# Macaron conformer / RG-LRU layer: a 128-column split at the entry of 256-column matmul runs, a fixed order for the first casts with idle matmuls on TensorE, and the quarter copies moved to a chain of lower priority

## The chip, the cores and the metric

The kernel runs on one core of one Trainium2 chip, as one launch. The metric is the device time of one execution in microseconds (us), median over runs. A separate profiled execution gives the trace; its span leaves out what lies before the first and behind the last instruction. Engines are named as in the profile: PE (TensorE matmul), PEld (TensorE weight load), DVE (VectorE), ACT (ScalarE), POOL (GpSimd), SP (the engine that issues most DMAs).

## The reference

One decoder layer on x of 512 tokens by 1024 features, float32, with three residual steps and a last norm:

```python
def swiglu_ffn(x, w_gate, w_up, w_down):
    return (jax.nn.silu(x @ w_gate) * (x @ w_up)) @ w_down

x = x + 0.5 * swiglu_ffn(rmsnorm(x, ffn1_norm), ...)     # 1024 -> 2816 -> 1024
x = x + hybrid_mixer(rmsnorm(x, mix_norm), ...)          # one 1024 -> 2048 input product
x = x + 0.5 * swiglu_ffn(rmsnorm(x, ffn2_norm), ...)
y = rmsnorm(x, final_norm)
```

The mixer splits its 2048 columns into four blocks of 512: value and gate of a causal depthwise convolution of width 31 (then a LayerNorm over channels and a silu), and input and gate of a linear recurrence over time (a convolution of width 4, two block-diagonal gates, a scan). Both halves go through one 1024 x 1024 output product.

## The kernel before

**Precision.** Every large product is made of three products in fp32r, a shorter float format of TensorE. An operand is split into `hi`, its value rounded to fp32r (a cast on ACT), and `lo`, the rest (a subtraction on DVE), and the sum is hi·hi + hi·lo + lo·hi. So each weight slab of 128 x 1024 that arrives by DMA (`raw`) costs a cast (line 203) and a subtraction (line 212) before PE can use it (`hl`), and each normed activation is transposed on PE (line 348, tile `ptr`), cast on ACT to `h_hi` (line 353) and subtracted on DVE to `h_lo` (line 359).

**Stages.** Both feed-forward parts have 22 feature tiles j of 128 features. The first two are computed in two halves of 256 tokens (`early_units`, called A and B in the code), because the norm of the first 256 tokens is ready first; each half is 24 matmuls of 256 columns into `pgate` and 24 into `pup` (line 305). Then, in the first part only, tile 2 is computed over all 512 tokens. The tiles behind that are computed by a seven-product scheme over quarters of the operands (`seven_units`, line 314): gate and up weights are one 2 x 2 block matrix, tokens and features of the input the other, and seven block products of 12 matmuls with 256 columns each (tiles `px`, `pz`, `pw`) do the work of eight. It needs sums of the input's quarters (`quarters`, lines 363 to 377, and `sums`, line 381; tiles `a`, `s`, `sx`) and sums of the weight blocks (lines 226 to 230, tile `tt`). Tiles are in groups of 8, 8 and 6; behind each group comes the down product in matmuls of 512 columns (lines 520 to 522), and behind its first slab stand 12 matmuls of 256 columns that were held back from the last tile (`late`). The mixer's input product (`zc_units`) begins with two column blocks in halves of 256 tokens and goes on with 512 columns.

**Order.** The work is a list of units. `run` goes through the list; for each unit it first issues what lies ahead by fixed distances (`AHEAD`: loads 8 slabs ahead, casts 4, subtractions 3), then the unit's matmuls, then one step of every side chain (norms, sums of quarters), then the unit's evacuation. The framework then orders each engine's queue by priority, in which `high_priority(offset=...)` moves a piece forward; `keep_in_program_order` pins an instruction to the place where it is written. Each engine runs its queue strictly in order. A norm is a chain (`norm_chain`): squares with a running sum on ACT (line 324), two small operations on POOL (lines 325 and 328), the scaling on DVE (line 340 for the first norm, where the gain is broadcast by a matmul with one row, `g`, line 893; line 334 for the later ones), then transposes, casts, subtractions and, for the two feed-forward norms, the copies for the quarters' sums. Tokens are in four tiles t of 128; the first norm handles t = 0 and 1 ahead of the list and t = 2 and 3 in a chain.

Of the kernel before, what the change touches and what calls it, by code (L numbers as in the profile page):

```python
# [8 lines left out]
F32 = mybir.dt.float32  # L9
# [19 lines left out]
BESIDE = (4, 5, 6, 9, 11, 13, 15, 18, 20)  # L29
ASIDE = 16  # L30
TAPS = 31
PR_NORM = 800
# [18 lines left out]
class Slab:  # L51
    def __init__(self, src=None, split=None, home=None, off=0):
        self.src, self.split, self.home, self.off = src, split, home, off


# [17 lines left out]
def layer_kernel(ctx: ExitStack, tc, x, gains, w_g1, w_u1, w_d1a, w_d1b, w_in,  # L73
# [119 lines left out]
    def slab_hi(s):  # L193
        if isinstance(s, Block):
            block_hi(s)
            return
        if s.home is not None:
            s.hi, s.lo = s.home()
        else:
            hl = hl_tile(s.off)  # L200
            s.hi, s.lo = hl[:, 0:D], hl[:, D:2 * D]
        if s.split is None:
            S.copy(s.hi, s.raw)  # L203
        elif s.home is not None:
            nc.sync.dma_start(s.hi.bitcast(F32), s.split[:, 0, :])
            nc.sync.dma_start(s.lo.bitcast(F32), s.split[:, 1, :])
        else:
            nc.sync.dma_start(hl.bitcast(F32).rearrange("p (s d) -> p s d", s=2), s.split)

    def slab_lo(s):  # L210
        if s.split is None:
            V.tensor_sub(s.lo, s.raw, s.hi.bitcast(F32))  # L212
            dve(1.15)


# [24 lines left out]
    def run(units):  # L240
# [8 lines left out]
        for i, u in enumerate(units):  # L249
            while used < len(order) and first[order[used]] <= i:  # L250
                used += 1
            for stage in range(3):
                while put[stage] < min(used + AHEAD[stage], len(order)):
                    s = order[put[stage]]
                    if stage == 0:
                        slab_load(s)
                    elif stage == 1:
                        if live >= HL_BUFS and put[1] >= used and s.home is None:
                            break
                        slab_hi(s)  # L260
                        live += s.home is None
                    else:
                        if put[2] >= put[1]:
                            break
                        slab_lo(s)
                    put[stage] += 1
# [32 lines left out]

    def mm_feat(ps, s, t0, n):  # L300
        hi = s.hi.rearrange("p (k f) -> p k f", k=KT)
        lo = s.lo.rearrange("p (k f) -> p k f", k=KT)
        for i, (w, h) in enumerate(((hi, h_hi), (hi, h_lo), (lo, h_hi))):
            for k in range(KT):
                PE.matmul(ps, w[:, k, :], h[:, k, t0:t0 + n],  # L305
                          start=(i == 0 and k == 0), stop=(i == 2 and k == KT - 1))

    def mm_block(ps, b, a, first):  # L310
        (whi, wlo), (hhi, hlo) = b, a
        for i, (w, h) in enumerate(((whi, hhi), (whi, hlo), (wlo, hhi))):
            for k in range(4):
                PE.matmul(ps[:, 0:HT], w[:, k * P:(k + 1) * P], h[:, k, :],  # L314
                          start=(first and i == 0 and k == 0), stop=(i == 2 and k == 3),
                          skip_group_check=not first)

# [3 lines left out]
    def norm_stats(t):  # L321
        xn = slot([P, D], "xn")
        ss = sp.tile([P, 16], F32, name=nm("ss"), tag="ss", bufs=4)
        S.activation(xn, xt[t], AF.Square, scale=1.0 / 32.0, accum_out=ss[:, 0:1])
        ins = G.tensor_scalar_add(ss[:, 0:1], ss[:, 0:1], RMS_EPS)
# [5 lines left out]
    def norm_scale(t, xs, g):  # L331
# [6 lines left out]
        for oh in range(2):  # L338
            sl = slice(oh * 512, (oh + 1) * 512)
            V.scalar_tensor_tensor(out=xn[:, sl], in0=xt[t][:, sl], scalar=ss[:, 1:2],  # L340
                                   in1=g[oh], op0=ALU.mult, op1=ALU.mult)

    def transposed(t, xs):
        pts = []
        for hf in range(2):
            pt = bank("ptr").rearrange("p (a b) -> p a b", a=4)
            for k in range(4):
                ins = PE.transpose(pt[:, k, :], xs[0][:, (hf * 4 + k) * P:(hf * 4 + k + 1) * P],
                                   ident)
                if pinned[0]:  # L350
                    tc.keep_in_program_order(ins)
            dst = (slice(None), slice(hf * 4, hf * 4 + 4), slice(t * P, (t + 1) * P))
            S.copy(h_hi[dst], pt)
            pts.append((pt, dst))
        return pts

    def transposed_lo(pts):
        for pt, dst in pts:
            V.tensor_sub(h_lo[dst], pt, h_hi[dst].bitcast(F32))
            dve(0.66)  # L360


    def quarters(t, pts, q):
# [4 lines left out]
        if t < 2:  # L368
            S.copy(q["a11"][at], p0)
            S.copy(q["a12"][at], p1)  # L370
        else:
# [4 lines left out]
        if t == 3:  # L376
            chains.append((PR_COMB, sums(q)))


# [19 lines left out]

    def norm_chain(ts, g, key=None, q=None):  # L400
        xs = [norm_stats(t) for t in ts]
        for t, x_ in zip(ts, xs):
            norm_scale(t, x_, g)
        yield 1
        for t, x_ in zip(ts, xs):
# [3 lines left out]
            if q is not None:  # L409
                quarters(t, p, q)  # L410
        if key is not None:
# [7 lines left out]

    def ffn_units(acts, j, g, u_, parts):  # L420
        off = ASIDE if len(parts) == 2 else 0
        sg_, su_ = Slab(g, off=off), Slab(u_, off=off)
        box = {}

        def product(key, s, t0, n):
            box[key] = bank("p" + key)
            mm_feat(box[key][:, :n], s, t0, n)

# [12 lines left out]
        for t0, n in parts:  # L441
            us = 5.44 * n / 512
            out_.append(Unit([sg_], us, lambda t0=t0, n=n: product("gate", sg_, t0, n),
                             lambda t0=t0, n=n: gate_out(t0, n), n == T))
            out_.append(Unit([su_], us, lambda t0=t0, n=n: product("up", su_, t0, n),
                             lambda t0=t0, n=n: up_out(t0, n), n == T))
# [4 lines left out]

    def seven_units(acts, j, g, u_, q):
        pair = {"gate": g, "up": u_}
# [6 lines left out]
        def product(to, b, a, first):  # L460
# [3 lines left out]
            sl = slice(i * HALF, (i + 1) * HALF)  # L464
            mm_block(box[to], (blk.hi[:, sl], blk.lo[:, sl]), q[a], first)

# [47 lines left out]
    def early_units(acts, wg, wu, between):  # L514
        e = [ffn_units(acts, j, wg[j], wu[j], [A, B]) for j in range(2)]
        return e[0][:2] + e[1][:2] + between + e[0][2:] + e[1][2:]

# [81 lines left out]
    def zc_units(c, parts):  # L599
# [4 lines left out]
        def product(key, s, t0, n):  # L604
            box[key] = bank("pz")
            mm_feat(box[key][:, :n], s, t0, n)

# [259 lines left out]
    def softplus_consts():  # L867
# [4 lines left out]
        V.tensor_max(e, lam, na)  # L872
        S.activation(e, e, AF.Exp, scale=-1.0)
        V.tensor_scalar_add(s, e, 2.0)
# [13 lines left out]

    row1 = sp.tile([1, P], F32, name="row1", tag="sg", bufs=2)
    V.memset(row1, 1.0)  # L890
    g1ps = [bank("g1") for _ in range(2)]
    for oh in range(2):
        PE.matmul(g1ps[oh], row1, grow[:, cols(oh)], start=True, stop=True)
    gains_of = {}
# [33 lines left out]
    def rest_of_x():  # L928
        for t in (2, 3):
            nc.sync.dma_start(xt[t], x[t * P:(t + 1) * P, :])  # L930
        chains.append((PR_FIRST, norm_chain((2, 3), g1ps, "h11", q1)))

# [8 lines left out]
    def ffn(a0, wg, wu, wd, q, plain, between=()):  # L941
# [8 lines left out]
        for gi, n in enumerate(GROUPS):  # L950
            for i in range(n):
# [9 lines left out]
                m = seven_units(acts[gi], i, wg[j], wu[j], q)  # L961
                m[4].aside = j in BESIDE
# [14 lines left out]
    e = early_units(a1, w_g1, w_u1, wait("h11"))  # L977
    u = e[:1] + do(rest_of_x) + e[1:]
    u += do(lambda: sides.append(split_ahead(for_later, ws_in + ws_out)))
# [121 lines left out]
```

## Time and profile before

| | |
|---|---|
| median of 3 runs | 871.55 us (870.31 to 871.9) |
| profiled execution, its own time | 874.41 us |
| its span | 872.4 us |
| PE busy | 849.3 us, 97% |
| DVE busy | 638.0 us, 73% |
| ACT busy | 425.6 us, 49% |
| DMA | 139.12 MB, mean 159 GB/s |

PE is busy nearly throughout, so what counts is how long its matmuls take and where it waits. Two things are to be kept in mind. A matmul's row in the timeline shows its start and a length that overlaps with the next one: the cost of a matmul in a dense run is the distance of its start to the next start, not its length. And the row "PEclk" is the clock that the throttle granted.

The list of engine queues that is shown beside the profile's rows tells which instruction stands where in its engine's queue; it has no times.

### The profile page before, as it was taken

What the parts mean: (1) busy time and instruction counts of PE and PEld (TensorE: products, weight loads), DVE (VectorE), ACT (ScalarE), POOL (GpSimd) and SP (SyncE); (2) the same over time, 40 slices, a digit from 0 to 9 for tenths busy, and PEclk for the clock granted to TensorE, in tenths of its full rate; (3) what the DMA queues carried; (4) which work ended last, traced back from release to release, by engine and by line L of the source; (5) the groups of instructions that cost most, each with busy time, mean ns of one, the idle gap of its engine ahead of it and who ended that gap; (6) DMA issues with size and microseconds to landing.
All of it is one profiled execution on the core that took longest, in us unless ns stands there. A gap on an engine that the chain in (4) does not pass through costs nothing.

```text
span 872.4 us, 13745 instructions
## 1 busy us (share of the span) xinstructions
PE 849.3 (97%) x5568; PEld 772.7 (89%) x5568; DVE 638.0 (73%) x899; ACT 425.6 (49%) x677; POOL 89.6 (10%) x112
## 2 busy tenths in 40 slices
PE   7999999999999999999996999999999999999996
PEld 5999988999889998998783889999889999899985
DVE  5989765997668984569897669796547994558844
ACT  7656533556435652435742545555225654135633
POOL 2000010000110000209820010000000000000001
PEclk9999999999999999999997999999999999999999
DMA  7536895555885569655451021234312335223312
GB/s 283 150 138 241 286 323 212 179 184 171 293 308 196 191 234 369 218 201 185 146 193 48 26 72 51 96 121 125 120 49 95 111 110 166 74 73 98 104 43 96
DMA packets 36721, 139.12 MB, mean 159 GB/s; under 512 B 5041, under 2 KB 5169, under 8 KB 33970
## 3 DMA queue, kind: packets, MB, share of 16 engines
q1 hardware_dynamic: 29170, 112.04, 38.3%
q0 software_dynamic: 6912, 25.17, 7.5%
q8 instruction: 43, 0.70, 0.3%
q10 hardware_dynamic: 576, 1.05, 0.3%
q14 instruction: 20, 0.16, 0.1%
HBM read 110.98 MB, written 27.26 MB: 158 GB/s over the span
## 4 chain that ended last, share of the span: by engine, by line
PE 91%; DVE 4%; ACT 3%; DMA 1%; issue 1%; POOL 0%; SPq 0%; POOLq 0%; ACTq 0%; DVEq 0%
PE px L314 25%; PE pz L314 13%; PE pd L521 8%; PE pd L520 8%; PE pd L522 8%; PE pz L305 7%; PE pw L314 6%; PE pgate L305 3%; PE pup L305 3%; DVE pc L660 2%; PE po L520 1%; PE po L522 1%; PE po L521 1%; PE pdl L520 1%; PE pdl L521 1%; PE pdl L522 1%
## 5 line engine op out<-in xcount | busy, mean ns | idle before, releaser
L212 DVE TENSOR_TENSOR hl<-raw,hl 128x1024 fp32r<-128x1024 f32 (+1 forms) x132 | 139.9, 1063 | 45.2 <-ACT hl L203 33.1
L314 PE MATMUL px<-sx,hl 128*128 128x256 f32 x936 | 123.0, 281 | 0.0
L314 PE MATMUL pz<-sx,hl 128*128 128x256 f32 x936 | 123.0, 281 | 0.0
L212 DVE TENSOR_TENSOR hl<-tt,hl 128x1024 fp32r<-128x1024 f32 x78 | 95.0, 1218 | 35.0 <-ACT hl L238 34.9
L520 PE MATMUL pd<-hl,act 128*128 128x512 f32 x304 | 118.7, 390 | 0.0
L521 PE MATMUL pd<-hl,act 128*128 128x512 f32 x304 | 118.5, 390 | 0.0
L522 PE MATMUL pd<-hl,act 128*128 128x512 f32 x304 | 118.4, 389 | 0.0
L314 PEld LDWEIGHTS px<-sx,hl 128*128 128x128 f32 x936 | 115.8, 189 | 0.0
L314 PEld LDWEIGHTS pz<-sx,hl 128*128 128x128 f32 x936 | 115.7, 189 | 0.0
L314 PE MATMUL px<-h_hi,hl 128*128 128x256 f32 x624 | 98.7, 281 | 0.0
L238 ACT CAST hl<-tt 128x1024 fp32r<-128x1024 f32 x78 | 81.9, 1053 | 28.1 <-PE pd L522 18.4
L314 PEld LDWEIGHTS px<-h_hi,hl 128*128 128x128 f32 x624 | 84.9, 189 | 1.1 <-DVE um L492 0.4
L238 ACT CAST hl<-raw 128x1024 fp32r<-128x1024 f32 x78 | 65.2, 835 | 38.9 <-PE pd L522 30.8
L203 ACT CAST hl<-raw 128x1024 fp32r<-128x1024 f32 x54 | 56.1, 1052 | 51.7 <-PE pd L522 41.1
L522 PEld LDWEIGHTS pd<-hl,act 128*128 128x128 f32 x304 | 57.1, 188 | 11.9
L520 PEld LDWEIGHTS pd<-hl,act 128*128 128x128 f32 x304 | 57.1, 188 | 11.6
L521 PEld LDWEIGHTS pd<-hl,act 128*128 128x128 f32 x304 | 57.1, 188 | 11.3
L305 PE MATMUL pz<-h_hi,hl 128*128 128x512 f32 (+1 forms) x320 | 64.9, 352 | 0.0
L305 PEld LDWEIGHTS pz<-h_hi,hl 128*128 128x128 f32 x320 | 51.8, 188 | 9.2 <-issue 1.9
L660 DVE SCALAR_TENSOR_TENSOR pc<-sx,ch,pc 128x512 f32<-128x512 f32 x84 | 56.9, 749 | 0.0
L291 DVE TENSOR_TENSOR slo<-sraw,shi 128x1024 fp32r<-128x1024 f32 x24 | 29.3, 1222 | 29.6 <-ACT shi L290 29.5
L498 DVE TENSOR_TENSOR sg<-sg,um 128x512 f32<-128x512 f32 x39 | 27.0, 691 | 32.5 <-ACT sg L497 32.5
(181 smaller groups left out, 1348.4 us busy)
## 6 DMA issues: line engine op xcount, KB each, us to landing
raw<-in_w_g SPq DMA_DIRECT2D x44, 512.0 KB, 3.6
raw<-in_w_u SPq DMA_DIRECT2D x44, 512.0 KB, 3.6
hl<-wsi SPq DMA_DIRECT2D x16, 1024.0 KB, 4.8
sraw<-in_w_in SPq DMA_DIRECT2D x16, 512.0 KB, 6.2
wsi<-shi POOLq DMA_DIRECT2D x16, 512.0 KB, 5.9
wsi<-slo POOLq DMA_DIRECT2D x16, 512.0 KB, 5.0
raw<-in_w_d1a SPq DMA_DIRECT2D x16, 512.0 KB, 4.4
raw<-in_w_d2a SPq DMA_DIRECT2D x16, 512.0 KB, 3.5
```

The source lines that it names most:

```text
L203: S.copy(s.hi, s.raw)
L212: V.tensor_sub(s.lo, s.raw, s.hi.bitcast(F32))
L238: S.copy(s.hi, s.raw)
L291: V.tensor_sub(lo, raws[-1], hi.bitcast(F32))
L305: PE.matmul(ps, w[:, k, :], h[:, k, t0:t0 + n], start=(i == 0 and k == 0), stop=(i == 2 and k == KT - 1))
L314: PE.matmul(ps[:, 0:HT], w[:, k * P:(k + 1) * P], h[:, k, :], start=(first and i == 0 and k == 0), stop=(i == 2 and k == 3), skip_group_ch ...
L498: V.tensor_mul(s, s, box["m"])
L520: PE.matmul(ps, ahi, whi, start=first, stop=False)
L521: PE.matmul(ps, ahi, wlo, start=False, stop=False)
L522: PE.matmul(ps, alo, whi, start=False, stop=last)
L660: V.scalar_tensor_tensor(out=o if j == TAPS - 2 else to, in0=src, scalar=par(c, P_DW + j), in1=to, op0=ALU.mult, op1=ALU.add)
```

## The change

- `mm_feat` and `mm_block` take a `cut`. Where it is 128, the second of the hi·hi matmuls (k = 1) is issued as two matmuls of 128 columns with the same weights in place of one of 256. It is given at 12 places: the first gate product of each half of the early tiles (both feed-forward parts), the first gate product of each half in the mixer, and the first seven-product block of each group.
- At the beginning, a 128 x 128 tile of ones (`warm`) takes the place of the row of ones; 7 idle matmuls on it are issued ahead of the gain's broadcast, and three times 3 more: behind the broadcast, behind the transposes of t = 0 and behind those of t = 1. Their result is not used.
- A silu on 16 columns that nobody reads is the first activation.
- The first norm's instructions and the first casts and subtractions of weights are pinned in the order in which they are now written: both halves of t = 0, then of t = 1; casts of `h_hi` ahead of the weights' casts; squares of t = 2 and 3 ahead of the copies for the quarters.
- The copies and sums of `quarters` are no longer part of the norm's chain (priority 800 or 50) but a chain of their own with the priority of the sums (0).
- The second tile's up product over the first half is two units (hi·hi, then the rest), and the cast distance is 3 slabs in place of 4 for the first 5 units. The exponential among the mixer's constants is pinned.

```diff
@@ run
-                while put[stage] < min(used + AHEAD[stage], len(order)):
+                while put[stage] < min(used + AHEAD[stage] - (stage == 1 and i < 5),
+                                       len(order)):
...
@@ mm_feat, mm_block
+    def mm_feat(ps, s, t0, n, cut=0, passes=(0, 1, 2)):
...
+            for k in range(KT) if i in passes else ():
+                for c0, c1 in pieces(n, cut if i == 0 and k == 1 else 0):
+                    ins = PE.matmul(ps[:, c0:c1], w[:, k, :], h[:, k, t0 + c0:t0 + c1],
+                                    start=(i == 0 and k == 0), stop=(i == 2 and k == KT - 1))
...
+    def pieces(n, cut):
+        return ((0, cut), (cut, n)) if cut else ((0, n),)
...
+                for c0, c1 in pieces(HT, cut if i == 0 and k == 1 else 0):
+                    PE.matmul(ps[:, c0:c1], w[:, k * P:(k + 1) * P], h[:, k, c0:c1],
+                              start=(first and i == 0 and k == 0), stop=(i == 2 and k == 3),
+                              skip_group_check=not first)
...
@@ norm_chain
             transposed_lo(p)
             if q is not None:
-                quarters(t, p, q)
+                chains.append((PR_COMB, quarter_chain(t, p, q)))
...
@@ early_units, zc_units, ffn
+        e = [ffn_units(acts, j, wg[j], wu[j], [A, B], CUT if j == 0 else 0) for j in range(2)]
+        return e[0][:2] + e[1][:3] + between + e[0][2:] + e[1][3:]
...
+            mm_feat(box[key][:, :n], s, t0, n, CUT if key == "g" and c == 0 else 0)
...
+                m = seven_units(acts[gi], i, wg[j], wu[j], q, CUT if i == 0 or j == plain else 0)
...
@@ the beginning
+    warm = const([P, P], "warm")
+    V.memset(warm, 1.0)
+    junk = sp.tile([P, 16], F32, name=nm("ss"), tag="ss", bufs=4)
+    pin(S.activation(junk, warm[:, 0:16], AF.Silu))
+    idle = bank("idle")
+    def keep_busy(n):
+        for _ in range(n):
+            pin(PE.matmul(idle[:, 0:P], warm, warm, start=True, stop=True))
+    keep_busy(IDLE[0])
...
-    for _ in norm_chain((0, 1), g1ps, None, q1):
-        pass
+    xs = [norm_stats(t) for t in range(2)]
...
+    rest_of_x()
+    keep_busy(IDLE[1])
+    norm_scale(0, xs[0], g1ps)
+    norm_scale(1, xs[1], g1ps)
+    pts = []
+    for t in range(2):
+        pts.append(transposed(t, xs[t]))
+        keep_busy(IDLE[2 + t])
+        pin(slab_hi(firsts[t]))
+    xs2 = [norm_stats(t) for t in (2, 3)]
+    for p in pts:
+        transposed_lo(p)
+    for k in range(2):
+        pin(slab_lo(firsts[k]))
+        firsts[k].put = 3
+    quarters(0, pts[0], q1)
+    pin(slab_hi(firsts[2]))
+    firsts[2].put = 2
+    quarters(1, pts[1], q1)
```

Where the change moves instructions, the engines' queues show it. PE from the program's beginning, before (line 893 is the gain's broadcast, `ptr` the transposes):

```order
L893 MATMUL g_1_90<-grow,row_88 128x512
L893 MATMUL g_2_91<-grow,row_88 128x512
L348 MATMUL ptr_140<-ident,xn_126 128x128 x4
L348 MATMUL ptr_146<-ident,xn_126 128x128 x4
L348 MATMUL ptr_158<-ident,xn_131 128x128 x4
L348 MATMUL ptr_164<-ident,xn_131 128x128 x4
L305 MATMUL pgate_204<-h_hi,hl_190 128x256 x4
L305 MATMUL pup_234<-h_hi,hl_192 128x256
L305 MATMUL pgate_204<-h_hi,hl_190 128x256 x4
```

and the same place with the change:

```order
L936 MATMUL idle_92<-warm 128x128 x7
L941 MATMUL g_3_100<-grow,warm 128x512
L941 MATMUL g_4_101<-grow,warm 128x512
L936 MATMUL idle_92<-warm 128x128 x3
L369 MATMUL ptr_163<-ident,xn_136 128x128 x4
L369 MATMUL ptr_169<-ident,xn_136 128x128 x4
L936 MATMUL idle_92<-warm 128x128 x3
L369 MATMUL ptr_180<-ident,xn_141 128x128 x4
L369 MATMUL ptr_186<-ident,xn_141 128x128 x4
L936 MATMUL idle_92<-warm 128x128 x3
L316 MATMUL pgate_233<-h_hi,hl_178 128x256
L316 MATMUL pgate_233<-h_hi,hl_178 128x128 x2
```

Sixteen idle matmuls are added, and the second gate matmul is in two pieces.

PE where the first group of seven-product tiles begins, behind the 512-column up product of tile 2, before:

```order
L305 MATMUL pup_546<-h_hi,hl_400 128x512 x8
L314 MATMUL px_588<-h_hi,hl_433 128x256 x4
L314 MATMUL px_588<-h_lo,hl_433 128x256 x4
L314 MATMUL px_588<-h_hi,hl_433 128x256 x4
L314 MATMUL pz_606<-sx_52_461,hl_472 128x256 x12
```

and with the change, from the second matmul of that block on:

```order
L331 MATMUL px_609<-h_hi,hl_452 128x128 x2
L331 MATMUL px_609<-h_hi,hl_452 128x256 x2
L331 MATMUL px_609<-h_lo,hl_452 128x256 x4
L331 MATMUL px_609<-h_hi,hl_452 128x256 x4
L331 MATMUL pz_628<-sx_58_514,hl_487 128x256 x12
```

Only the one matmul is split; the order behind it is the same.

ACT around the transposes of t = 2 in the second feed-forward part's norm (the last ACTIVATE on `xt_72` is the squares of t = 3), before:

```order
L353 CAST h_hi<-ptr_5078 128x4x128
L353 CAST h_hi<-ptr_5084 128x4x128
L372 COPY s_654_5123<-ptr_5084 128x4x128
L431 ACTIVATE sg_5134<-pgate_5096 128x256
L324 ACTIVATE xn_5128,ss_5129<-xt_72 128x1024
L436 CAST act_5176<-sg_5134 128x256
```

and with the change:

```order
L373 CAST h_hi<-ptr_5098 128x4x128
L373 CAST h_hi<-ptr_5104 128x4x128
L341 ACTIVATE xn_5150,ss_5151<-xt_72 128x1024
L398 COPY s_663_5198<-ptr_5104 128x4x128
L462 ACTIVATE sg_5156<-pgate_5122 128x256
L373 CAST h_hi<-ptr_5186 128x4x128
```

The squares of t = 3 now stand ahead of the copy for the quarters and of the gate's silu.

More of the change, by code (lines that the diff above doesn't have):

```diff
@@ L53, in __init__ @@
         self.src, self.split, self.home, self.off = src, split, home, off
+        self.put = 0
 class Block:
@@ L202, in slab_hi @@
         if s.split is None:
-            S.copy(s.hi, s.raw)
+            return S.copy(s.hi, s.raw)
         elif s.home is not None:
@@ L303, in mm_feat, with mm_block @@
         for i, (w, h) in enumerate(((hi, h_hi), (hi, h_lo), (lo, h_hi))):
[L304 to L310, printed above, removed]
+            for k in range(KT) if i in passes else ():
+                for c0, c1 in pieces(n, cut if i == 0 and k == 1 else 0):
+                    ins = PE.matmul(ps[:, c0:c1], w[:, k, :], h[:, k, t0 + c0:t0 + c1],
+                                    start=(i == 0 and k == 0), stop=(i == 2 and k == KT - 1))
+                    if passes[0] == i == 1 and k == 0:
+                        tc.keep_in_program_order(ins)
+    def pieces(n, cut):
+        return ((0, cut), (cut, n)) if cut else ((0, n),)
+    def mm_block(ps, b, a, first, cut=0):
         (whi, wlo), (hhi, hlo) = b, a
@@ L349, in transposed @@
                                    ident)
-                if pinned[0]:
-                    tc.keep_in_program_order(ins)
+                tc.keep_in_program_order(ins)
             dst = (slice(None), slice(hf * 4, hf * 4 + 4), slice(t * P, (t + 1) * P))
-            S.copy(h_hi[dst], pt)
+            ins = S.copy(h_hi[dst], pt)
+            if not pinned[0]:
+                tc.keep_in_program_order(ins)
             pts.append((pt, dst))
@@ L358, in transposed_lo @@
         for pt, dst in pts:
-            V.tensor_sub(h_lo[dst], pt, h_hi[dst].bitcast(F32))
+            ins = V.tensor_sub(h_lo[dst], pt, h_hi[dst].bitcast(F32))
+            if not pinned[0]:
+                tc.keep_in_program_order(ins)
             dve(0.66)
@@ L368, in quarters @@
         if t < 2:
-            S.copy(q["a11"][at], p0)
-            S.copy(q["a12"][at], p1)
+            for key, pt in (("a11", p0), ("a12", p1)):
+                ins = S.copy(q[key][at], pt)
+                if not pinned[0]:
+                    tc.keep_in_program_order(ins)
         else:
@@ L886, in softplus_consts @@
         V.tensor_scalar_mul(nsp, q, -8.0)
-    row1 = sp.tile([1, P], F32, name="row1", tag="sg", bufs=2)
-    V.memset(row1, 1.0)
+    pin = tc.keep_in_program_order
+    warm = const([P, P], "warm")
[7 more added lines that the diff above has]
+    keep_busy(IDLE[0])
     g1ps = [bank("g1") for _ in range(2)]
     for oh in range(2):
-        PE.matmul(g1ps[oh], row1, grow[:, cols(oh)], start=True, stop=True)
+        pin(PE.matmul(g1ps[oh], warm[0:1, :], grow[:, cols(oh)], start=True, stop=True))
     gains_of = {}
```

70 lines of the change are left out of this document (44 added, 26 removed).

## The prediction

> **What bounds the kernel.** The page comes first, for the engine that sets the time.
>
> ```profile
> span 872.4 us, 13745 instructions
> PE 849.3 (97%) x5568; PEld 772.7 (89%) x5568; DVE 638.0 (73%) x899; ACT 425.6 (49%) x677; POOL 89.6 (10%) x112
> PE 91%; DVE 4%; ACT 3%; DMA 1%; issue 1%; POOL 0%; SPq 0%; POOLq 0%; ACTq 0%; DVEq 0%
> ```
>
> PE is 91% of the chain that ended last, so a gain must come from what a matmul costs or from PE's few gaps. The second view is therefore PE's timeline, read by the distance of starts.
>
> ```profile
> 13.49 1.22 PE L305 MATMUL pgate<-h_hi,hl 128*128 128x256 f32 x4 [0.85 <-ACT h_hi L353]
> ...
> 15.58 1.91 PE L305 MATMUL pgate<-h_lo,hl 128*128 128x256 f32 x8
> 17.28 1.81 PE L305 MATMUL pgate<-h_hi,hl 128*128 128x256 f32 x8
> 18.93 0.97 PE L305 MATMUL pup<-h_hi,hl 128*128 128x256 f32 x7
> ...
> 24.27 1.03 PE L348 MATMUL ptr<-ident,xn 128*128 128x128 f32 x8
> 25.07 1.19 PE L305 MATMUL pup<-h_hi,hl 128*128 128x256 f32 x8
> 26.09 1.10 PE L305 MATMUL pup<-h_lo,hl 128*128 128x256 f32 x8
> 27.03 1.11 PE L305 MATMUL pup<-h_hi,hl 128*128 128x256 f32 x8
> 27.98 1.03 PE L348 MATMUL ptr<-ident,xn 128*128 128x128 f32 x8
> 29.25 0.73 PE L305 MATMUL pgate<-h_hi,hl 128*128 128x256 f32 x4 [0.24 <-ACT h_hi L353]
> ...
> 34.81 1.07 PE L305 MATMUL pgate<-h_hi,hl 128*128 128x256 f32 x8
> ...
> 39.34 1.07 PE L305 MATMUL pup<-h_hi,hl 128*128 128x256 f32 x8
> 40.25 1.09 PE L305 MATMUL pgate<-h_hi,hl 128*128 128x512 f32 x4
> ```
>
> The same matmul of 256 columns has three prices. From 15.58 to 17.28, eight take 1.70 us: 213 ns each. From 34.81 to 40.25, 48 take 5.44 us: 113.3 ns. From 26.09 to 27.98, sixteen take 1.89 us: 118 ns. The first is a cold array; the other two are two paces of a warm one. Which of the two the long stretches have is a question for the sums by stretch, here the seven-product line alone (PE and PEld: busy time and count):
>
> ```profile
> 51.20:99.20 48.00, 48.00 (x408) 47.97 (x407) 1.00 0.57 201
> ...
> sum 377.20, PE 377.09 PEld 376.86; mean PE 62.85 PEld 62.81
> ```
>
> Six stretches hold 3204 matmuls (408, 660, 492, 492, 660, 492) in 377.2 us: 117.7 ns, the slower pace, with no gap in it. They are 43% of the span. Both PE and the weight loads are busy throughout, so a matmul there waits for its own load: pace is set between the two.
>
> **Is the pace a state?** Each run keeps the pace it begins with: 3204 never leave 117.7, and the run from 29.25 to 40.25 keeps 113.3 over semaphore waits and a change of tile. So what decides is the entry. Entries from 512 columns and from transposes (25.07) all fell into the slower pace. The run at 29.25 began behind a stall, with the array waiting for its first load, and fell into the faster. Two short entries, each behind a pair of 512-column matmuls and a wait for weights, tell how fine this is:
>
> ```profile
> 325.84 0.64 PE L314 MATMUL px<-h_lo,hl 128*128 128x256 f32 x4
> 326.31 0.64 PE L314 MATMUL px<-h_hi,hl 128*128 128x256 f32 x4
> 832.18 0.62 PE L314 MATMUL px<-h_lo,hl 128*128 128x256 f32 x4
> 832.63 0.62 PE L314 MATMUL px<-h_hi,hl 128*128 128x256 f32 x4
> ```
>
> The first stays slow (0.47 us for four), the second turns fast (0.45). Both paces can thus be reached from the same program place; a disturbance that leaves the array waiting for a load can flip it.
>
> **The change, part by part.**
>
> *Cuts (12).* A half of 128 columns streams in half the time but still brings a whole weight load, so behind it the array waits for a load, which is what the two entries into the fast pace (29.25, 832) had and the entries from 512 columns lacked. The first sign is therefore in favour; against it stands the entry at 25.07, where 128-column transposes lead into the slow pace (these stream float32 and keep the array busy: eight from 24.27 to 25.07 are 100 to 109 ns each). I take it that the cuts work. Gain: 3204 x (117.7 − 113.3) = 14.1 us. Of the early and mixer halves 288 more lie behind a cut (144 in the second feed-forward part, 144 in the mixer): 1.3 us. Some 5 matmuls per entry are not yet at pace, as from 29.25: 12 x 5 x 4.4 ns = 0.3 us lost. Bounds: 0 if no entry flips, 15.4 if all do.
>
> *Price of a cut.* No fp32r matmul of 128 columns is in the trace. From below: the pair for the price of one, 0. The nearest row is the transposes: 2 x 109 − 118 = 100 ns. From above, plain float32 (line 893, quoted next): 3.75 us for two products of 512 columns in four rows, so 0.47 us per 128 columns cold, 0.25 warm, a cut at 0.38 us. I take 0.1, since load time is what a half cannot fall below: 12 x 0.1 = 1.2 us (0 to 4.6).
>
> The Trainium skill, "TensorE: Matmul & The Clock Gate", sections on the back-to-back issue gap and on the weight-path modes, speaks against these terms: it gives one warm spacing, columns over 2.4 GHz plus 2.5 ns, 109 ns at 256 columns, and a load of 128 columns at 107 ns that float32 cannot shorten. By it there is no second pace to win and a pair of halves costs two loads. The trace disagrees on the first (113.3 and 117.7 stand side by side) and agrees on the second (transposes at 109).
>
> *The beginning.* PE, DVE and ACT up to the first gate matmul, and the last of the quarters' sums:
>
> ```profile
> 4.09 3.75 PE L893 MATMUL g<-grow,row 1*128 1x512 f32 x4 [4.09 <-DMA grow<-in_gains]
> 9.82 2.82 PE L348 MATMUL ptr<-ident,xn 128*128 128x128 f32 x12 [0.94 <-DVE xn L340]
> 8.36 2.06 DVE L340 SCALAR_TENSOR_TENSOR xn<-xt,ss,g 128x512 f32<-128x512 f32 x3 [1.22 <-POOL ss L328]
> 12.81 1.95 DVE L359 TENSOR_TENSOR h_lo<-ptr,h_hi 128x512 fp32r<-128x512 f32 x3
> 14.68 3.49 DVE L212 TENSOR_TENSOR hl<-raw,hl 128x1024 fp32r<-128x1024 f32 x3
> 10.93 1.05 ACT L203 CAST hl<-raw 128x1024 fp32r<-128x1024 f32 x1
> 12.83 1.09 ACT L353 CAST h_hi<-ptr 128x512 fp32r<-128x512 f32 x2
> 16.16 1.12 ACT L324 ACTIVATE xn<-xt 128x1024 f32<-128x1024 f32 x1
> 43.09 1.22 DVE L390 TENSOR_TENSOR sx<-a,sx 128x1024 fp32r<-128x1024 f32 x1
> ```
>
> DVE scales t = 1 before the second half of t = 0, so three scalings follow 8.36; with the new order only two do (end near 10.0 with the broadcast's end at 7.84 in front). Four transposes (0.5) and one cast (0.58) later, and with no weight cast of 1.05 between, the gate starts near 11.3 in place of 13.49: 2.2 us. The idle matmuls fill PE from about 1.2 us on, so I take the array as warm by then: the first 25 matmuls, 13.49 to 18.93, would take 2.8 in place of 5.4 us: 2.6. The gap ahead of 29.25 (1.27 us from 27.98, for eight transposes of 0.87) goes, since those transposes now come earlier: 0.4. A faster PE meets DVE sooner: four `h_lo` (0.65 each) and a weight's subtraction (1.16) end near 13.8, the second near 15, with PE due at 13.6 and 16.3; with the casts further on, 0.9 us of new waits. Net 4.3 us. The last sum of quarters ends at 44.3 today, 7 us ahead of the first stretch at 51.2, so an arrival 4 us earlier is covered.
>
> If the array stays cold, nine idle matmuls (0.47 each) stand between broadcast and gate: 7.8 + 9 x 0.47 + 16 transposes at 0.22 = 15.5, 2.0 us late. So the term is −4.9 to +2.0.
>
> *Copies at a lower priority.* They matter in the second feed-forward part:
>
> ```profile
> 522.17 1.07 ACT L353 CAST h_hi<-ptr 128x512 fp32r<-128x512 f32 x2 [1.22 <-PE ptr L348]
> 524.88 0.59 ACT L372 COPY s<-ptr 128x512 f32<-128x512 f32 x1 [1.64 <-DVE h_lo L359]
> 525.71 1.05 ACT L324 ACTIVATE xn<-xt 128x1024 f32<-128x1024 f32 x1
> 522.37 0.68 DVE L526 SCALAR_TENSOR_TENSOR xt<-po,xt 128x512 f32<-128x512 f32 x1
> 528.31 1.28 DVE L334 SCALAR_TENSOR_TENSOR xn<-xt,ss,gbc 128x1024 f32<-128x1024 f32 x1 [0.46 <-POOL ss L328]
> 529.74 1.06 PE L348 MATMUL ptr<-ident,xn 128*128 128x128 f32 x8 [1.52 <-DVE xn L334]
> ```
>
> The residual of t = 3 is ready at 523.05, but its squares stand behind a copy in which ACT waits 1.64 us for DVE, and start at 525.71. PE then waits 1.52 us. With the squares ahead of the copy they start behind the casts of `h_hi`, near 523.3, 2.4 us sooner, and the wait of 1.52 is covered: −1.5 (0 to −1.5). The first activation and the moved exponential lie on ACT, which is 49% busy: nothing, and 0.2 at most.
>
> *Sum* against the profiled 874.41: −14.1 − 1.3 + 0.3 + 1.2 − 4.3 − 1.5 = −19.7, so 854.7. The median of the runs is 2.9 us lower, 871.55; the sum there is **852**.
>
> **Rivals.**
>
> *The pace stays.* The cuts cost 1.2 and win nothing; 4.3 and 1.5 remain: −4.6, **867**. For it: all entries from 512 columns and from transposes are slow today, and the entry behind a wait at 325 as well. Against: two of the three entries behind a wait are fast. The one spacing of the skill's page would lead here.
>
> *Half the runs flip.* Each long run is its own draw, or a short wait flips one back: DVE is 43.05 us busy of 48.00 in the first stretch, 93% of what remains at the faster pace:
>
> ```profile
> 51.20:99.20 48.00, 48.00 (x409) 48.00 (x408) 43.05 (x75) 32.88 (x54) 3.19 (x6) 1.00 0.57 201
> ```
>
> Half of 15.4 is lost: **859**.
>
> *The beginning becomes later.* Mechanism: what is pinned stands ahead of what PE needs. Idle matmuls in a cold array put the gate 2.0 us later, and ACT, which must now finish the squares of t = 3 before the third weight's cast, waits for that DMA: today the squares of t = 2 run at 16.16 without a wait, so the bytes are there by then; in the new order the squares of t = 3 are due about 1.5 us sooner, and that is the most that ACT can lose. With the copies' 1.5 and the cuts' price of 1.2 that makes +3.2: **875**. It decides the sign only where the pace stays. For it: the broadcast and the transposes, 3.75 and 2.82 us of PE, did not warm the array. Against: the idle matmuls use all 128 rows, the broadcast one.
>
> **How the numbers follow.** Forecast 0.62, pace stays 0.20, half 0.10, later beginning 0.05, no visible effect 0.03 (the pace stays and cuts at their upper price, 4.6, use up 4.3 and a part of 1.5). The forecast's own range, from all bounds at their good end (−14.1 − 1.3 − 4.9 − 1.5 = −21.8, 850) to a dear cut and a poor start, is 849 to 857. With the two rivals at 859 and 867 the range is 849 to 868; what lies above is 0.08. A measurement tells 0.2%, 1.7 us, from no change: faster 0.91, same 0.03, slower 0.06.
>
> **What would show it.** The seven-product stretches should read 113 ns per matmul (408 in 46.2 us); the first gate matmul near 11.3 us with 113 ns at once; the 512-column gate near 36 in place of 40.25; no wait ahead of the transposes near 529.74; a pair of halves near 0.22 us. The forecast is wrong if the stretches still read 117.7, or if DVE shows waits inside them.

## The result, and the profile after

| | before | changed kernel |
|---|---|---|
| median | 871.72 us (870.31 to 874.34, 4 runs) | 857.82 us (857.21 to 858.1, 4 runs) |
| profiled execution, its span | 874.41, 872.4 us | 858.1, 856.1 us |

The ratio is 0.9836 (95%: 0.9812 to 0.986): 13.9 us less. The forecast was 852, 19.7 less. The page of the changed kernel: span, busy time of the engines, and the chain that ended last.

```profile
span 856.1 us, 13844 instructions
PE 839.2 (98%) x5612; PEld 762.9 (89%) x5612; DVE 636.7 (74%) x899; ACT 424.7 (50%) x677; POOL 89.5 (10%) x112
PE 93%; DVE 4%; ACT 1%; DMA 0%; issue 0%; POOLq 0%; SPq 0%; POOL 0%; ACTq 0%
```

PE is still the bound, with 10.1 us less of busy time; the other 6.2 of the 16.3 us of span are time in which it stood. The six seven-product stretches, in the sums by stretch for the seven-product line (PE and PEld: busy time and count):

```profile
50.14:96.52 46.38, 46.38 (x409) 46.34 (x408) 1.00 0.63 222
141.51:216.45 74.94, 74.94 (x661) 74.90 (x660) 1.00 0.52 179
...
sum 364.01, PE 364.00 PEld 363.79; mean PE 60.67 PEld 60.63
```

They took 377.2 us and take 364.0: 13.2 less, cuts included (each stretch has one matmul record more). The beginning, in PE's timeline:

```profile
1.04 3.36 PE L936 MATMUL idle<-warm 128*128 128x128 f32 x14 [1.04 <-DVE warm L928]
4.48 3.78 PE L941 MATMUL g<-grow,warm 1*128 1x512 f32 x4
8.19 1.65 PE L936 MATMUL idle<-warm 128*128 128x128 f32 x6
9.63 1.92 PE L369 MATMUL ptr<-ident,xn 128*128 128x128 f32 x8
11.33 1.49 PE L936 MATMUL idle<-warm 128*128 128x128 f32 x6
12.61 1.71 PE L369 MATMUL ptr<-ident,xn 128*128 128x128 f32 x8
14.16 0.83 PE L936 MATMUL idle<-warm 128*128 128x128 f32 x6
14.75 1.29 PE L316 MATMUL pgate<-h_hi,hl 128*128 128x256 f32 x9
...
39.23 1.09 PE L316 MATMUL pgate<-h_hi,hl 128*128 128x512 f32 x4
```

Six records of idle products (two records for one product) take 1.65 and 1.49 us behind the broadcast and 0.83 at the end: the array was at half rate, 213 ns from start to start in place of some 110, until about 14.0 us. The gate starts 1.26 us *later* than before (13.49), then runs at full rate at once (at the slower pace, 118 ns, in spite of its cut), and the 512-column gate comes at 39.23 instead of 40.25. The whole beginning is worth 1.0 us. In the second feed-forward part:

```profile
513.82 1.04 PE L369 MATMUL ptr<-ident,xn 128*128 128x128 f32 x8
514.62 1.29 PE L316 MATMUL pgate<-h_hi,hl 128*128 128x256 f32 x9
515.75 1.11 PE L316 MATMUL pgate<-h_lo,hl 128*128 128x256 f32 x8
516.69 1.10 PE L316 MATMUL pgate<-h_hi,hl 128*128 128x256 f32 x8
...
520.46 1.03 PE L369 MATMUL ptr<-ident,xn 128*128 128x128 f32 x8
521.25 1.19 PE L316 MATMUL pgate<-h_hi,hl 128*128 128x256 f32 x8
```

The transposes at 520.46 have no wait ahead of them (1.52 us before). But the cut at 514.62 did not do its work: eight products from 515.75 take 0.94 us, 118 ns each, and the uncut run from 521.25 is at 118 too until the next cut.

So by marks of the two traces the span's 16.3 us are: 1.0 up to the 512-column gate, 13.2 in the six stretches, 0.3 in the mixer, 1.9 between the transposes at 513.82 and the second part's first seven-product block, less 0.1 behind the last stretch. Three questions stay: what each part does alone, why the beginning gave 1.0 instead of 4.3, and why the gain on the medians (13.9) is smaller than that on the profiles (16.3).

### The profile page after: what moved, and what is told of

The parts are those of the page before. It is cut to its first block, busy times and chain, and to the rows that moved or that the text cites. A ratio compares the mean times of both kernels' runs of the same rounds, so it can differ in the third digit from the quotient of the medians.

```text
span 856.1 us, 13844 instructions
## 1 busy us (share of the span) xinstructions
PE 839.2 (98%) x5612; PEld 762.9 (89%) x5612; DVE 636.7 (74%) x899; ACT 424.7 (50%) x677; POOL 89.5 (10%) x112
## 4 chain that ended last, share of the span: by engine, by line
PE 93%; DVE 4%; ACT 1%; DMA 0%; issue 0%; POOLq 0%; SPq 0%; POOL 0%; ACTq 0%
PE px L331 25%; PE pz L331 12%; PE pd L557 8%; PE pd L558 8%; PE pd L559 8%; PE pz L316 7%; PE pw L331 6%; PE pgate L316 3%; PE pup L316 3%; DVE pc L697 2%; PE po L557 2%; PE po L558 2%; PE po L559 2%; PE ptr L369 1%; PE pdl L559 1%; PE pdl L558 1%
## 5 line engine op out<-in xcount | busy, mean ns | idle before, releaser
L331 PE MATMUL px<-sx,hl 128*128 128x256 f32 x936 | 118.8, 276 | 0.0
L331 PE MATMUL pz<-sx,hl 128*128 128x256 f32 x936 | 118.8, 276 | 0.0
L331 PEld LDWEIGHTS px<-sx,hl 128*128 128x128 f32 x936 | 111.9, 188 | 0.0
L331 PEld LDWEIGHTS pz<-sx,hl 128*128 128x128 f32 x936 | 111.9, 188 | 0.0
L316 PE MATMUL pz<-h_hi,hl 128*128 128x512 f32 (+2 forms) x322 | 64.8, 350 | 0.0
L299 ACT CAST shi<-sraw 128x1024 fp32r<-128x1024 f32 x24 | 25.3, 1052 | 49.0 <-DMA sraw<-in_w_in 26.0
```

Of the source, the lines that this page charges most:

```text
L299: S.copy(hi, raws[-1])
L316: ins = PE.matmul(ps[:, c0:c1], w[:, k, :], h[:, k, t0 + c0:t0 + c1], start=(i == 0 and k == 0), stop=(i == 2 and k == KT - 1))
L331: PE.matmul(ps[:, c0:c1], w[:, k * P:(k + 1) * P], h[:, k, c0:c1], start=(first and i == 0 and k == 0), stop=(i == 2 and k == 3), skip_gro ...
```

## The experiments

### The cuts alone, and all but the cuts

The kernel before with the 12 cuts and nothing else:

```diff
-            for k in range(KT):
-                PE.matmul(ps, w[:, k, :], h[:, k, t0:t0 + n], ...)
+            for k in range(KT):
+                for c0, c1 in pieces(n, cut if i == 0 and k == 1 else 0):
+                    PE.matmul(ps[:, c0:c1], w[:, k, :], h[:, k, t0 + c0:t0 + c1], ...)
...
```

> The kernel before with the 12 cuts alone; beginning, copies and order as before. Theory (the cuts set the pace): the six seven-product stretches read 113 ns per matmul in place of 117.7, 13 to 14 us less, so about 857.5 us. Rival (the pace comes from the new order of the beginning): stretches stay at 117.7 and 12 cuts at 0.05 to 0.1 us each make about 872.5 us.

The changed kernel without its cuts:

```diff
-CUT = 128
+CUT = 0
```

> The changed kernel without the cuts. Theory: stretches at 117.7 ns, about 857.8 + 14 = 871.5 us, less if the beginning is worth more than the trace of one run shows. Rival: stretches stay at 113, about 857 us.

Cuts alone: 860.44 us (860.09 to 861.17), ratio 0.9873 (0.9851 to 0.9894). All but the cuts: 870.84 (868.68 to 871.71), ratio 0.9974 (0.9959 to 0.999). The sums over the same six stretches, first with the cuts alone, then without cuts:

```profile
sum 364.06, PE 364.02 PEld 363.83; mean PE 60.67 PEld 60.64
```

```profile
sum 377.41, PE 377.33 PEld 377.16; mean PE 62.89 PEld 62.86
```

Of the parts of this change, the cuts by themselves set the pace of the six stretches. The 860.44 is 3 us more than the 857.5 expected; against the profiled 874.41 the traced execution (860.19) is the expected 14 us faster, and the rest is the offset between profile and median that a later section follows. That PE's two paces can be chosen by a split is shown for an entry from 512 columns (five in each of four traces without cuts, all at 118; the same five in each of nine traces with cuts, all at 113) and for a split in the midst of a run at 118. In two of these nine the last 72 products of one stretch fell back to 118, 0.3 us. Why a split leads into the faster pace was argued in the prediction (the array waits for a load) and wasn't measured apart.

### Is the cut's price 0.1 us, and does a cut set the pace or turn it over?

A cut in all 273 seven-product blocks instead of 6:

```diff
-                     cut if b == "B11" else 0)
+                     cut)
...
-                m = seven_units(acts[gi], i, wg[j], wu[j], q, CUT if i == 0 or j == plain else 0)
+                m = seven_units(acts[gi], i, wg[j], wu[j], q, CUT)
```

> The changed kernel with the cut on every one of the 273 seven-product products instead of 6 of them: 267 more cuts. It prices a cut by itself and tells whether a cut sets the fast pace or turns one pace into the other. Theory (sets; a pair takes 61 + 110 = 171 ns where a whole product takes 118, so 0.053 us a cut more): 267 x 0.053 = +14.2, median 872 (870.5 to 874), all products at 113 apart from the cut ones. Price as predicted (0.1 us a cut): +26.7, 884.5. Rival (a cut turns the pace over): every other product at 117.7, 273 / 2 x 12 x 4.4 ns = +7.2 on top, 879. Rival (each cut is followed by about six products at 117 to 123 ns before the pace settles): 6 x 5 ns x 267 = +8 on top, 880.

Measured 891.7 us (889.94 to 892.03), ratio 1.0211 (1.0188 to 1.0234). My expectation of 872 was wrong. The first two stretches:

```profile
49.45:100.01 50.56, 50.56 (x442) 50.52 (x441) 1.00 0.62 204
145.08:226.86 81.78, 81.78 (x715) 81.74 (x714) 1.00 0.47 154
```

Against 46.38 and 74.94 us they have 33 and 54 records more, and 4.18 and 6.84 us: 0.127 us for each, and 267 x 0.127 = 33.9, all of the difference to 857.8. The starts around one cut are 57, 112 and 170 ns apart, then 117, 119, 116, 114, and then 113 again until the next. I had counted 61 + 110 for the pair and had overlooked that the product *behind* the pair starts late as well: the two halves and what follows hold 0.113 us, the settling 0.014. The pace behind each cut is 113 again, so a cut sets it and doesn't turn it over. The prediction's 0.1 a cut with 0.025 for settling was right within 2 ns. The three starts hold 339 ns together, as much as three whole products at 113: that fits its ground, that a half costs a whole load, though the pair itself takes 0.169 us and not the 0.22 that was to be seen.

### Is it the idle matmuls that made the beginning late?

```diff
-IDLE = (7, 3, 3, 3)
+IDLE = (0, 0, 0, 0)
```

> The changed kernel without its 16 idle matmuls. Theory (the array stays cold until about 14 us whether or not they are there, and they hold up the transposes): first gate matmul near 12 us in place of 14.75, then up to 5 us at 213 ns; the time is within 1.5 us of 857.8 and differs more from run to run, since the moment at which the array turns warm is not tied to the program. Rival (they are what warms the array and pay for it): 2.5 us slower, 860 or more.

856.37 us (855.73 to 857.58), ratio 0.9825 (0.9805 to 0.9845): 1.4 less than the changed kernel. PE's timeline:

```profile
7.91 3.73 PE L369 MATMUL ptr<-ident,xn 128*128 128x128 f32 x16
12.05 2.29 PE L316 MATMUL pgate<-h_hi,hl 128*128 128x256 f32 x9 [0.40 <-ACT h_hi L373]
```

The fixed order brings the gate to 12.05, where the idle products had it at 14.75. It then runs at half rate until 16.5, and still the 512-column gate is earlier: 38.10 against 39.23. So in these traces the order is worth 2.1 us of the beginning, and the idle products took back 1.1 of it; part of the 2.1 is that half rate ended earlier than in the trace of the kernel before (16.5 against 18.85).

### Does the array leave half rate at the same moment each time?

The trace of the variant without cuts has the same instructions as the changed kernel up to the first gate product, but another time of them:

```profile
4.14 1.98 PE L941 MATMUL g<-grow,warm 1*128 1x512 f32 x4
...
7.36 1.97 PE L369 MATMUL ptr<-ident,xn 128*128 128x128 f32 x8 [0.37 <-DVE xn L359]
9.12 1.49 PE L936 MATMUL idle<-warm 128*128 128x128 f32 x6
10.40 1.20 PE L369 MATMUL ptr<-ident,xn 128*128 128x128 f32 x8
...
12.02 1.17 PE L316 MATMUL pgate<-h_hi,hl 128*128 128x256 f32 x8
```

The broadcast takes 1.98 us instead of 3.78: half rate ended at 3.9 us, and the 512-column gate comes at 36.97. That is 3.3 us earlier than before, of the 4.3 forecast. But it came back: the transposes from 7.36 and the idle products from 9.12 are 213 ns apart again. In the sums by stretch of this trace, the granted clock (the figure ahead of the last two) is 1.00 from 3.89 to 7.30 and then half:

```profile
7.30:10.71 3.41, 3.35 (x16) 3.36 (x17) 3.26 (x5) 1.94 (x3) 0.45 (x1) 0.50 1.00 395
```

From 10.71 on it is 1.00 again, in time for the gate. In the trace of the variant with the copies put back (below) half rate likewise ends at 4.26, returns at 7.68 and ends again at 11.09. The variant without cuts also shows two groups of times: four of its ten executions take 868.7 to 869.3 us, the traced one among them, and six take 870.8 to 871.7. Three kernels were run on this. The changed kernel again:

> The changed kernel unaltered, in more executions. What it tells apart is why the beginning gave 1.0 us instead of 4.3. Theory: the array leaves its half rate at a moment that differs between executions of the same program. In the traces with the same beginning it was about 4.1 us from the span's start in two (second layer entry, pgate on 512 columns, at 36.97 and 36.70) and about 13.9 us in one (39.23); so the times should fall in two groups about 2.3 us apart, one near 857.8 and one near 855.5, with little between, and a median anywhere from 855.5 to 858. Rival: the beginning of the changed kernel always is as in its profile, and the two others were early because of their other edits; then all times lie within 857.2 to 858.1 as in the four before, in one group.

857.79 us (857.89, 855.79, 857.83, 857.75): seven of eight executions of the changed kernel lie within 857.2 to 858.1 and one 2.0 us lower, with nothing between. That fits the two moments; the low one left no trace, so for it this is inferred. All idle products in front, and the same with one row:

```diff
-IDLE = (7, 3, 3, 3)
+IDLE = (16, 0, 0, 0)
```

> The changed kernel with all idle products ahead of the gain's broadcast: 16 there (32 records, 6.8 us at 213 ns, from 1.04 to 7.9 us), none between the transposes. Theory A (the array leaves half rate after some stretch of unbroken full-width products of at most 6.8 us): half rate ends between 4.1 and 7.9 us in every execution, broadcast in 2.0 us instead of 3.8, gate between 12.3 and 14.3 us, the 512-column gate between 36.9 and 38.9, times in one group, median 856 (854.8 to 857.2). Rival B (the moment has nothing to do with the idle products): half rate ends near 13 to 17 us, the broadcast and the transposes start 3.6 us later than in the variant without idle products, gate near 15.6, and the median is near 859.5.

```diff
-            pin(PE.matmul(idle[:, 0:P], warm, warm, start=True, stop=True))
+            pin(PE.matmul(idle[:, 0:P], warm[0:1, :], warm[0:1, :], start=True, stop=True))
```

> As the variant with 16 idle products in front, but each idle product uses one row of the array (1 by 128 with 1 by 128) instead of 128. Theory A' (products on one row don't count for leaving half rate; in the trace of before the gain's broadcast, also of one row, took 3.75 us from 4.09 and half rate lasted until 18.85): half rate lasts through the idle products and the broadcast, gate near 15.6 us, the 512-column gate near 40.5 to 42, median 859.5 (858.5 to 861). Rival B' (every product counts alike): as with full idle products, median 856 and half rate over by 7.9 us.

Sixteen full idle products: 856.51 us (855.42 to 857.32); sixteen with one row: 859.5 (859.37 to 860.77). The beginning of the first and then of the second:

```profile
1.04 5.95 PE L936 MATMUL idle<-warm 128*128 128x128 f32 x32 [1.04 <-DVE warm L928]
6.92 1.98 PE L941 MATMUL g<-grow,warm 1*128 1x512 f32 x4
...
12.51 1.30 PE L316 MATMUL pgate<-h_hi,hl 128*128 128x256 f32 x9 [0.79 <-ACT h_hi L373]
```

```profile
1.04 7.19 PE L936 MATMUL idle<-warm 1*128 1x128 f32 x32 [1.04 <-DVE warm L928]
8.03 3.62 PE L941 MATMUL g<-grow,warm 1*128 1x512 f32 x4
...
15.71 1.65 PE L316 MATMUL pgate<-h_hi,hl 128*128 128x256 f32 x6 [0.40 <-ACT h_hi L373]
```

Full products end half rate at 5.5 us; products on one row of the array keep it busy just as long (213 ns a record) and half rate lasts until 20.1 us, 4.4 us behind the first gate product. Both medians and moments came out as expected, though the times with full products spread over 1.9 us instead of forming one group. PE being busy is not what counts. That also fits the changed kernel: the 3.7 us behind the first seven idle products are the broadcast, a product of one row.

The Trainium skill ("TensorE: Matmul & The Clock Gate", section on the HAM clock gate) gives about 3.4 us of sustained activity, seen through a window that runs freely, and a moment that varies by half a microsecond. The window agrees with the traces: the changes at 3.89, 7.30 and 10.71 lie 3.41 us apart, as do those at 4.26, 7.68 and 11.09. The spread is wider here: with the changed kernel's beginning half rate first ended at 3.9 and 4.3 us in two traces and at 12.4 to 14.0 in three others.

An estimate from all 13 traces joins these moments. They are 18.85, 19.08 and 18.26 (the kernel before), 16.89 (cuts alone), 16.50 (no idle products), 20.14 (one row), 13.98, 13.63, 12.36, 4.26 and 3.89 (the changed kernel's beginning), 5.50 (16 in front) and 12.09 (the last variant below). Go back from each in steps of 3.41 us and count 213 ns for each start on 128 rows, whether idle product, transpose or gate product. The last step then holds some 2.7 us or more in every trace, and no earlier step more than some 2.55. By that the first idle products, 14 x 0.213 = 3.0 us, are sometimes enough and sometimes not, as a step happens to begin. The transposes and gate products from 7.91 in the variant without idle products, with a wait of 0.40 us among them, just missed one step and filled the next, at 16.5. This share was read from the moments afterwards; no run varies it, and it doesn't say when half rate returns.

### Are the copies at lower priority worth 1.5 us?

The changed kernel with the copies and sums of quarters back in the norm's chain:

```diff
-                chains.append((PR_COMB, quarter_chain(t, p, q)))
+                quarters(t, p, q)
```

> The changed kernel with the quarters' copies back in the norm's chain. Theory: the 1.5 us wait of PE ahead of the transposes of t = 3 in the second feed-forward part returns: 859.3 us. Rival (the wait went because PE now comes at another time): no wait there, 857.8 us.

856.92 us (856.75 to 858.71), not slower than the changed kernel. The trace shows why the total doesn't answer:

```profile
4.33 1.98 PE L941 MATMUL g<-grow,warm 1*128 1x512 f32 x4
...
12.07 1.29 PE L316 MATMUL pgate<-h_hi,hl 128*128 128x256 f32 x9
...
519.61 1.06 PE L369 MATMUL ptr<-ident,xn 128*128 128x128 f32 x8 [1.60 <-DVE xn L353]
```

This execution first left half rate at 4.3 us and was at full rate for the gate, so its beginning is 2.5 us shorter (512-column gate at 36.70 against 39.23), and the wait of 1.60 us is back in the second part. From the 512-column gate to the product behind these transposes it takes 483.73 us, against 482.02 in the changed kernel: beginning aside, the wait removed is worth about what it was costed at, 1.5 us. On the medians it is hidden by the beginning's spread.

### Where the 2.9 us between the profile and the median went

The forecast was summed against the profiled 874.41 and then lowered by 2.9, to the median. Two more traces of the kernel before, unaltered:

> The kernel before, unaltered, with a trace of another execution: its times run from 869.5 to 875.9, far wider than the 855.8 to 858.1 of the changed kernel, and the profiled one (874.41) lay 2.9 us above the median from which the forecast was taken. Theory: entries of runs behind the transposes fall into the fast pace in some executions and into the slow in others; the run of 636 products at 530.56, all at 117.8 in the profiled execution, is 636 x 4.45 = 2.8 us shorter where it falls into the fast one. An execution near 871.5 has that run at 113.3 (or stretches of about that number), one above 873.5 has none. Rival: the executions differ in the beginning alone (the moment at which the array leaves half rate, 18.85 us in the profiled one); then every stretch has 117.8 and the first seven-product product starts as much earlier than 51.16 as the time is below 874.4.

> A third traced execution of the kernel before, to the same question. Theory: its time equals 874.4, less 4.45 ns for each product of a stretch that is at 113.3 instead of 117.8 (2.8 us for the 636 behind 530.56), less what the beginning is earlier than 51.16 at the first seven-product product; the first of these two parts is not zero in executions below 872. Rival: the first part is zero, the second carries all.

They took 872.01 and 871.6 us. Of the first: the sums for its first stretch and for that of the second part (seven-product line), and PE's timeline at the transposes ahead of the latter's run:

```profile
51.58:99.63 48.05, 48.05 (x408) 48.01 (x407) 1.00 0.56 199
547.31:603.16 55.85, 55.76 (x492) 55.81 (x492) 1.00 0.32 104
```

```profile
530.16 1.07 PE L348 MATMUL ptr<-ident,xn 128*128 128x128 f32 x8 [1.52 <-DVE xn L334]
530.98 1.17 PE L305 MATMUL pgate<-h_hi,hl 128*128 128x256 f32 x8
531.98 1.07 PE L305 MATMUL pgate<-h_lo,hl 128*128 128x256 f32 x8
532.89 1.07 PE L305 MATMUL pgate<-h_hi,hl 128*128 128x256 f32 x8
```

Of the second, the same sums:

```profile
51.18:99.23 48.05, 48.05 (x408) 48.01 (x407) 1.00 0.56 200
546.87:602.72 55.85, 55.76 (x492) 55.82 (x492) 1.00 0.32 104
```

In both, the stretch of 492 in the second part takes 55.85 us instead of the 57.95 of the profiled execution: 113.5 ns, without any cut, and so does the whole run of 636 matmuls that begins behind the transposes at 530 (eight from 531.98 in 0.91 us). That is 636 x 4.4 = 2.8 us. The other five stretches are at 117.8. For the first: 874.41 − 2.8 + 0.4 (its beginning is that much later, 51.58 against 51.16) = 872.0, as measured. The theory holds, and the rival (the beginning alone) falls: the beginnings differ by 0.4 us, and in the wrong direction. These 0.4 us are a pace too: in the first of these traces the run at 29.26, which the prediction read as fast because it begins behind a stall, begins behind the same stall and is slow (eight in 0.94 us, 96 x 4.4 ns = 0.4 us):

```profile
29.26 0.74 PE L305 MATMUL pgate<-h_hi,hl 128*128 128x256 f32 x4 [0.24 <-ACT h_hi L353]
...
31.96 1.10 PE L305 MATMUL pgate<-h_hi,hl 128*128 128x256 f32 x8
32.90 0.40 PE L305 MATMUL pup<-h_hi,hl 128*128 128x256 f32 x2
```

So, without a cut, the entries behind transposes fall either way in the same kernel, and a stall doesn't settle it.

The kernel before, then, has one of the six stretches at the better pace in two of three traced executions, those near its median; the cuts bring there what the profile shows less those 2.8 us. In five traces with the wait ahead of these transposes, two entries fell into the better pace; in eight traces of kernels without the wait, none. That is too few to show that the wait does it. It would fit that all of the change but the cuts is worth only 1.5 us (870.84 against 872.32 for the kernel before beside it): it takes away a wait of 1.5 us and, with it, perhaps the entry that saves 2.8.

### First idle products only, and a later cut

```diff
-IDLE = (7, 3, 3, 3)
+IDLE = (7, 0, 0, 0)
...
-                for c0, c1 in pieces(n, cut if i == 0 and k == 1 else 0):
+                for c0, c1 in pieces(n, cut if i == 0 and k == 3 else 0):
```

(the second in `mm_feat` alone)

> The changed kernel with idle products only in the first place (7, in the time in which PE waits for the gain's row; none between the transposes), and the cut of the first feed-forward product four products after the entry instead of two. Beginning, theory: what made the changed kernel's gate late (14.75) are the nine later idle products at half rate, so the gate starts at 12.1 to 12.4 whether half rate has ended or not, and the times lie at 854.5 to 855.5 (half rate over by 4.3 us) or 856 to 857 (not), median near 856.4, 1.4 below the changed kernel. Rival: the first idle products alone bring nothing and cost the 0.2 us that the broadcast waits for them, median 857 or more. Cut, theory: the cut two products behind an entry from transposes comes before the pace has settled and so is lost (514.84 stayed at 117.8 in four of four executions); four behind, that run falls to 113.3. Rival: the entry stays at 117.8 wherever the cut stands, since something else in it decides.

855.73 us (854.9 to 855.97), ratio 0.9803 (0.9773 to 0.9833): the lowest median here, 2.1 us under the changed kernel's, though the intervals of the two ratios overlap, and between the two groups that were expected. In its trace the 512-column gate comes at 37.02, 2.2 us ahead of the changed kernel's.

```profile
8.04 3.73 PE L369 MATMUL ptr<-ident,xn 128*128 128x128 f32 x16
12.17 1.31 PE L316 MATMUL pgate<-h_hi,hl 128*128 128x256 f32 x9 [0.40 <-ACT h_hi L373]
...
512.47 1.30 PE L316 MATMUL pgate<-h_hi,hl 128*128 128x256 f32 x9
513.61 1.07 PE L316 MATMUL pgate<-h_lo,hl 128*128 128x256 f32 x8
514.51 1.07 PE L316 MATMUL pgate<-h_hi,hl 128*128 128x256 f32 x8
```

The gate starts at 12.17, and in this execution at full rate. The entry at 512.47, cut four products behind the transposes, is at 113 ns (0.90 us for eight from 513.61), where the run with the cut two products behind was at 118 in all six traces with the changed kernel's order of copies. That the later cut did this is not shown by one trace: the same entry was at 113 without any cut in the variant without cuts and in the third trace of the kernel before, and at 118 in the other two of the kernel before. (With the old order of the copies and the earlier cut it was at 113 in two of two traces; what decides here is open.)

## Why the prediction was right or wrong

- **The pace** (−14.1, with settling and the price of the cuts −13.4 in the six stretches): right, 13.2 measured, by the cuts alone. The rivals "the pace stays" and "half the runs flip" fall. The ground given, that a stall at the entry leads into the faster pace, didn't hold: the run at 29.26 begins behind the same stall and is fast in two traces of the kernel before and slow in one. So the evidence for the cuts was weaker than it read, and that they worked was in part luck.
- **Price of a cut and settling** (0.1 us, 0.025): right, 0.127 together. The Trainium skill's warm spacing ("TensorE: Matmul & The Clock Gate", section on the back-to-back issue gap), which spoke against this, doesn't hold here: both paces, 113 and 118 ns, stand side by side in one kernel. That section gives its formula for a single matmul taken by itself, which the prediction left out, and says that in a stream the weight loads set the spacing too.
- **The shorter entries** (−1.3 for 288 matmuls): some 225 of the 288 reached 113 ns, 1.0 us; nearly all of the rest are the run at 514.62, which stayed at 118 behind its cut.
- **The copies** (−1.5): right in place and size; whether the removed wait also took a fast entry with it is open.
- **The beginning** (−4.3; 1.0 measured): the step that failed is "the idle matmuls fill PE from about 1.2 us on, so I take the array as warm by then". In both traces of the changed kernel the array was at half rate until 14 us, and the nine idle products that stand between broadcast and gate put the gate at 14.75, against 12.05 without them; the bound for a cold array had it at 15.5. What was still gained came from the gate products, which were at full rate at once. The other step, the gate 2.2 us earlier by the order, came to 1.4 (12.05, and 12.17 in the last variant, forecast 11.3) where these products are gone. This is 3.3 us of the miss.
- **From the profile to the median** (−2.9): the step "The median of the runs is 2.9 us lower; the sum there is 852" failed. The 2.9 us were not a constant offset but one run of 636 products that had the better pace already, which the cuts can't bring twice. The changed kernel's profile lies 0.3 us from its median. 852 + 3.3 + 2.9 = 858.2, against 857.82.

The direction was right, and so was the term on which 14 of the 20 us rested: pace is set at the entry and a split changes it. The forecast's own range, 849 to 857, missed the time by 0.8 us; it lies in the range of 849 to 868 only because that takes in two rivals that did not come true.

## What to carry to other kernels

Long runs of one matmul shape can lock into one of two paces at their entry, here 113 and 118 ns. Where the distance of starts shows the worse one, split one product near the entry, and not more often, since a split costs 0.127 us here. Behind products of 512 columns, and in the midst of a run, that worked each time; two products behind transposes (514.62) the run stayed at 118 in six of eight traces. Before a gain is carried from a profile to a median, ask which of its parts the median already has; and products that shall end half rate must fill the array and may not stand in the way of real work while they don't.

## What was not expected

- A run may gain where a stall stands ahead of it: behind the wait of 1.5 us at the transposes of the kernel before, the following 636 products were at the better pace in two of three traces, a gain of 2.8 us. That the stall is the cause is not shown.
- Products on one row of the array, back to back for 7.2 us, did not end half rate, where products on 128 rows ended it after 4.5 us.
- The granted clock shows a return to half rate (0.50 from 7.30 to 10.71 in the variant without cuts), but not the half rate in which the program begins. In the sums by stretch of the changed kernel it is 1.00 from 8.20 to 14.00, where the distance of starts shows half rate:

```profile
8.20:14.00 5.80, 5.80 (x28) 5.80 (x28) 3.45 (x5) 2.41 (x4) 0.00 (x0) 1.00 0.98 388
```

- With the same beginning, half rate ended for good at 10.7 us in one trace and at 14.0 in another, and the 512-column gate comes some 2 us earlier in the first.
